# Half of the weight remainders of the two token mixers computed on POOL instead of VectorE

## The chip, the cores and the metric

The kernel runs on one core of one Trainium2 chip. The metric is device time in microseconds (us) of one execution, the median of several runs; less is better. The profile names the engines PE (matrix products), PEld (its weight loads), DVE (VectorE), ACT (ScalarE), POOL (GpSimd) and SP (the queue that issues the DMAs).

## The reference

A decoder trunk of two layers on 256 tokens of width 1024, all in fp32. Each layer is a half-step gated feed-forward (FFN), a token mixer, and a second FFN; before each of the three stands an RMS norm whose gain, shift and output gate come from a conditioning vector.

```python
c_act = jax.nn.silu(c)
for l in range(DEPTH):                                   # DEPTH = 2
    mod = (c_act @ w_ada[l] + b_ada[l])[:, None, :]
    sh0, sc0, g0, sh1, sc1, g1, sh2, sc2, g2 = jnp.split(mod, N_MOD, axis=-1)
    h = _rmsnorm(x, norm_g[l, 0]) * (1.0 + sc0) + sh0
    x = x + 0.5 * g0 * _swiglu(h, ffn_w_gate[l, 0], ffn_w_up[l, 0], ffn_w_down[l, 0])
    h = _rmsnorm(x, norm_g[l, 1]) * (1.0 + sc1) + sh1
    x = x + g1 * _token_mix(h, w_in[l], w_out[l], ...)
    h = _rmsnorm(x, norm_g[l, 2]) * (1.0 + sc2) + sh2
    x = x + 0.5 * g2 * _swiglu(h, ffn_w_gate[l, 1], ffn_w_up[l, 1], ffn_w_down[l, 1])
return _rmsnorm(x, final_g)
```

`_token_mix` projects h by w_in, runs three groups of heads beside each other (a spatial gating unit, a differential attention, and a sparse attention with a compressed and two windowed branches), joins their outputs and projects them by w_out.

## The kernel before

Tokens lie on the free axis (256 of them), the model axis on the 128 partitions in 8 chunks. PE gets fp32 accuracy out of three float32r products: each weight tile comes from memory as a raw fp32 tile `wst`, ACT copies it to a float32r tile `wh` (line 207), and DVE subtracts the two (line 211) so that `wl` holds what the copy rounded away. A product of 128 output rows is then, for each of 8 chunks, wh times the high part of h, wh times its low part, and wl times the high part: 24 products of 256 columns. A weight tile is 128x1024 (512 KB) in most places; the values of the sparse attention use tiles of 840 and 560 columns (`w_in_vs`).

`split` issues the load, the copy and the subtraction. The pools let it run ahead of PE: 5 raw tiles, 6 wh, 6 wl. SP issues the loads in a fixed order, each when its raw tile is free, so when the subtraction that last read it is done.

Each mixer (`mix`) takes 29 splits: 14 tiles of w_in with weights stationary (`ws_u`, `ws_in`), 4 + 3 tiles with tokens on the partitions (`xs_in`), and 8 tiles of w_out. The order of PE within a mixer is written out by hand (`MIX_ORDER`, one list of parts per layer); the orders of DVE, ACT, POOL and SP are set by a scheduler when the program is built, and each engine runs its own list strictly in order. On DVE the mixer also does the softmax maxima and reciprocals (533, 541), the rotary sums (512, 522), the scalings of the probabilities (692 to 698, 906 to 917), the norm (272, 276), and `acc` (192, 194): the products of w_ada with the conditioning vector, a chunk of 128x512 at a time, which fill free places of DVE ahead of the next FFN. POOL does nothing after four small memsets at the start.

In the trace the first mixer lies at about 222 to 376 us and the second at 757 to 900. Both have the same three parts: a head (projections of the compressed branch, norm, values; to 252 and 788), a middle (attention; to 340 and 860), and the output projection at the end (`ps_out`).

Of the kernel before, what the change touches and what calls it, by code (L numbers as in the profile page):

```python
# [10 lines left out]
F32 = mybir.dt.float32  # L11
# [7 lines left out]
T = 256  # L19
# [16 lines left out]

# [1 line left out]
def _cols(spec):  # L38
    off, m = 0, {}
    for name, n in spec:  # L40
        m[name] = slice(off, off + n)
        off += n
    return m, off


NW = 16         # products that warm the tensor engine while the first loads arrive
BUFS = dict(acc=2, ad=4, sm=4, t1k=9, u=27, wh=6, wl=6, wst=5)
LATE = 4        # tiles of the first FFN that run before it loads modulation weights
# order of the parts of the token mixer, layer by layer
MIX_ORDER = ["""  # L50
# [7 lines left out]
"""]  # L58
NE = 2          # gate/up tiles (and pairs of w_in tiles) that run before the norm is known
NS = 7          # gate/up tiles of the first FFN that are accumulated while w_ada arrives  # L60
UW = 2 * T + 2
# [50 lines left out]
def trunk_kernel(ctx: ExitStack, tc: tile.TileContext, A, depth=DEPTH, nf=NF, fsplit=FSPLIT):  # L112
    nc = tc.nc
# [7 lines left out]
    up = pool("u", BUFS["u"])  # L121
# [5 lines left out]

# [1 line left out]
    par = sing.tile([P, depth * NLC + 16], F32, name="par")  # L129
# [4 lines left out]
    h = sing.tile([P, KD, 2 * T], F32R, name="h")  # L134
# [21 lines left out]

# [1 line left out]
    def ada_cols(l, m, ks, ps):  # L158
        dst = mod[l][:, m, ks]
        nc.vector.tensor_add(dst, ps, lp(l, "bada")[:, m * 8 + ks.start:m * 8 + ks.stop])  # L160
        s, kind = divmod(m, 3)
        if kind == 1:
            nc.vector.scalar_tensor_tensor(out=gs[l][:, s, ks], in0=dst, scalar=1.0,
                                           in1=lp(l, "ng")[:, s * 8 + ks.start:s * 8 + ks.stop],
                                           op0=ALU.add, op1=ALU.mult)
        elif kind == 2:
            nc.vector.tensor_scalar_mul(hg[l][:, s, ks], dst, 1.0 if s == 1 else 0.5)
# [29 lines left out]

# [1 line left out]
    def load(src, cols, pool=wst, tag="wst"):  # L199
        st = pool.tile([P, cols], F32, name="wst", tag=tag)  # L200
        nc.sync.dma_start(st, src)
        return st

    def split(src, cols, mid=None):
        st = load(src, cols)
        wh = whp.tile([P, cols], F32R, name="wh", tag="wh")
        nc.scalar.activation(wh, st, AF.Copy)  # L207
        if mid:
            mid()
        wl = wlp.tile([P, cols], F32R, name="wl", tag="wl")  # L210
        nc.vector.tensor_sub(wl, st, wh.bitcast(F32))  # L211
        return wh, wl
# [7 lines left out]

# [1 line left out]
    sqs = [None]  # L222
# [12 lines left out]

    # brings the table of Sqrt in behind an instruction
    def sqrt_table(after):
        warm = sm.tile([P, 1], F32, name="warm", tag="ub")
        with tc.issue_after(after.ins):
            nc.scalar.activation(warm, ones, AF.Sqrt)  # L240

    # 1/rms of every token, broadcast over the partitions
    def rms_tokens():
# [34 lines left out]

    # x * gain before the norm is known: parts of a chunk, and the shift as two more columns
    def u_shift(l, s):  # L280
        sh = mod[l][:, 3 * s, :]
        nc.scalar.activation(ut[:, :, T], sh, AF.Copy)
        nc.vector.tensor_sub(ut[:, :, T + 1], sh, ut[:, :, T].bitcast(F32))
# [6 lines left out]

    # W^T (x * gain) and, per row, W^T shift
    def ws_u(src):
        wh, wl = split(src, KD * P)
        ps = psm.tile([P, T + 2], F32, name="ps_wu", tag="mm")
        for k in range(KD):
            s = slice(k * P, (k + 1) * P)
            mm(ps, wh[:, s], ut[:, k, :T + 2], start=(k == 0), stop=False)
            mm(ps[:, :T], wh[:, s], ut[:, k, T + 2:], start=False, stop=False)
            mm(ps, wl[:, s], ut[:, k, :T + 2], start=False, stop=(k == KD - 1))
        return ps  # L300
# [7 lines left out]

    # out[128 rows of W, T] of W^T h: weights stationary
    def ws_h(ps, wh, wl, ncol=P):  # L310
# [21 lines left out]

# [1 line left out]
    def swiglu_mul(pg, pu, gb=None, ub=None, pool=tp, tag="t1k"):  # L334
# [19 lines left out]

    # the first gate/up tiles, chunk by chunk of the model axis as its modulation arrives
    def startup(ns):
# [36 lines left out]
        with tc.manual_schedule(engines={mybir.EngineType.PE, mybir.EngineType.DVE, mybir.EngineType.Activation}):  # L393
            wt = up.tile([P, 2 * T], BF16, name="wt", tag="u")
            nc.vector.memset(wt, 0.0)
            wps = psw.tile([P, 2 * T], F32, name="ps_warm", tag="w")
            for _ in range(NW):
                mm(wps, wt[:, :P], wt, True, True)
# [51 lines left out]
    def ffn(l, w, ada_f, ada_d, nxt):  # L450
# [3 lines left out]
        if l == 0 and w == 0:  # L454
            raw += startup(min(NS, nf))
            act = [None] * len(raw)
        else:
            rb = rms_rows()
            for k in range(KD):
                h_chunk(l, s, k, rb)  # L460
            for f in range(min(NE, nf)):
                pg, gb = apply_r(ws_u(gate[f]), rb)
                pu, ub = apply_r(ws_u(upw[f]), rb)
                act.append(swiglu(pg, pu, gb, ub))
        f0 = len(act)
        late = LATE if raw else 0
        slots = spread(ada_f, nf - f0 - late)
# [39 lines left out]

# [1 line left out]
    def rope_sum(dst, z, cos, sin, n=T, b=None):  # L509
# [19 lines left out]

    # exp of score segments [128, n, keys] in PSUM, with the sums of their rows  # L530
    def softmax_seg(ps, n, name):
# [12 lines left out]
    def mix(l, ada, nxt):  # L544
        WI = A["w_in_ws"]
        pse = [ws_u(WI[l, 0])]
        r = rms_tokens()
        pse.append(ws_u(WI[l, 1]))
        rb = rms_bcast(r)
        early = [apply_r(p, rb) for p in pse]  # L550
        for k in range(KD):
            h_chunk(l, 1, k, rb)
        early += [apply_r(ws_u(WI[l, n]), rb) for n in (12, 13)]
        lam_init = 0.8 - 0.6 * math.exp(-0.3 * l)
        # lambda of the differential attention, on every partition
        lt = sm.tile([P, 64], F32, name="lt", tag="lt", bufs=1)
# [27 lines left out]

        # -- projections, tokens on partitions --
        def xs_in(src, width, kspl):
# [16 lines left out]
        def rope_q(dst, n, cos, sin, zb=None):  # L603
            z, b = zb if zb else (ws_in(WI[l, n]), None)
            rope_sum(dst, z, cs(cos), cs(sin), b=b)

        def rope_k(tiles, n, cos, sin, sel0):
            t = tp.tile([P, T], F32, name="ksum", tag="t1k")
            rope_sum(t, ws_in(WI[l, n]), cs(cos), cs(sin))
            for e, (ku, g) in enumerate(tiles):  # L610
# [5 lines left out]

        # -- gate of the spatial gating unit (before the norm is known) --
        uu = unit("ug")
# [6 lines left out]

        # -- blocks of the compressed branch: columns (group, block), position code, position code --
        a_t = []
# [13 lines left out]

        # -- values of the differential attention, v of the gating unit --
        pss = xs_in(A["w_in_gd"][l], 512, (2, 2, 2, 2))
# [3 lines left out]
        for i in range(NI):  # L647
            v = dvu[:, i * T:(i + 1) * T]
# [15 lines left out]

        # -- differential attention --
        osb, da_p = [], []
# [91 lines left out]

        # -- spatial gating unit --
        def gating():  # L760
# [33 lines left out]

        # -- compressed keys and values --
        hsb, hid = [], []
# [38 lines left out]

        # -- sparse attention --
        qu = [unit("qn") for _ in range(2)]
# [3 lines left out]
        gate = sm.tile([P, NI, 24], F32, name="gate", tag="gate", bufs=1)  # L841
# [120 lines left out]
        def w_out(m, c0, c1):  # L962
            if c0 == 0:
                wh, wl = split(A["w_out"][l, m], KD * P)
                ps = psw.tile([P, T], F32, name="ps_out", tag="w")
                wo[m] = wh, wl, ps
            wh, wl, ps = wo[m]
            for c in range(c0, c1):
                s = slice(c * P, (c + 1) * P)
                mm(ps, wh[:, s], yt[c][:, :T], c == 0, False)  # L970
                mm(ps, wh[:, s], yt[c][:, T:], False, False)
                mm(ps, wl[:, s], yt[c][:, :T], False, c == KD - 1)
            if c1 == KD:
                return add_out(l, 1, m, ps, nxt, 1)
# [31 lines left out]
        for m in range(2, KD):  # L1006
            if ada:
                ada_next()
            if m == KD - 2:
                ada_flush()  # L1010
                sqrt_table(after)
                u_shift(*nxt)
            after = w_out(m, 0, KD)

# [1 line left out]
    def halves(l, ms):  # L1016
# [28 lines left out]

# [1 line left out]
def _w_in_columns():  # L1047
# [33 lines left out]
def _layout(inp, depth, nf):  # L1081
    g = {k: np.asarray(v) for k, v in inp.items()}
    ns = min(NS, nf)
    o = {}
# [57 lines left out]
```

## Time and profile before

| | |
|---|---|
| median of 3 runs | 1096.6 us (1095.26 to 1096.73) |
| span of the profiled execution, first to last instruction | 1093.7 us |
| median less span (the profiled execution's own time is not listed; this is taken as what lies around its span) | 2.9 us |
| first mixer, 222 to 376 | 154 us: DVE busy 130.8, ACT 106.2, PE 140.3 |
| second mixer, 757 to 900 | 143 us: DVE busy 118.7, ACT 101.4, PE 136.3 |
| subtraction of line 211 | 332 times, 391.0 us in all, 58 of them in the two mixers |

An engine's busy time is that in which at least one of its instructions ran. The times of PE overlap and their ends are modelled, so a high busy share of PE does not say that it had no room. Where the text speaks of the chain, it means the profile's chain of waits: followed back from the last instruction, at each step to what released it.

### The profile page before, as it was taken

To read this page: it belongs to the slowest core of one execution; us is meant where nothing else is said; L and a number is where in the kernel's file an instruction comes from. 1 tells how busy PE (TensorE), PEld (TensorE's weight loads), DVE (VectorE), ACT (ScalarE), POOL (GpSimd) and SP (SyncE) were. 2 spreads that over 40 slices of the span, in tenths; PEclk is the share of its full clock that TensorE was granted. 3 is DMA by queue.
4 is the path that set the end of the run, shared out by engine and by line. 5 is a ranking of instruction groups with operands and counts; after the bars stand their busy time and mean duration, and the time that the engine had idled before them with its cause. 6 is when DMAs were issued, how large, how long until landed. Compare 5 with 4: busy or idle time off the path is not lost.

```text
span 1093.7 us, 20684 instructions
## 1 busy us (share of the span) xinstructions
PE 1060.2 (97%) x7928; PEld 970.2 (89%) x7928; DVE 850.8 (78%) x1573; ACT 624.7 (57%) x1320; POOL 0.2 (0%) x4
## 2 busy tenths in 40 slices
PE   8999999998988999999999999999999999999997
PEld 5899998887775999999899999988787699999986
DVE  3479999767997999887879878786799878555563
ACT  4365545666675865554556555455867766454441
POOL 0000000000000000000000000000000000000000
PEclk8999999999998999999999999999999999999999
DMA  8868988944835679997866888785555145555551
GB/s 330 295 238 339 355 326 310 324 160 132 320 130 181 221 243 343 341 312 252 280 230 231 318 277 297 263 312 197 180 184 184 58 154 174 188 180 187 174 159 39
DMA packets 73827, 257.55 MB, mean 235 GB/s; under 512 B 8320, under 2 KB 9728, under 8 KB 73728
## 3 DMA queue, kind: packets, MB, share of 16 engines
q1 hardware_dynamic: 73728, 256.23, 67.3%
q8 instruction: 62, 1.02, 0.4%
q14 instruction: 37, 0.30, 0.1%
HBM read 255.14 MB, written 1.05 MB: 234 GB/s over the span
## 4 chain that ended last, share of the span: by engine, by line
PE 83%; DVE 10%; ACT 5%; issue 1%; DMA 1%; SPq 0%; DVEq 0%; ACTq 0%
PE ps_ws L219 41%; PE ps_dn L219 23%; PE ps_wu L219 5%; PE ps_fst L219 4%; PE ps_out L219 4%; DVE wl L211 2%; DVE rt L512 2%; PE ps_y L219 1%; DVE mx L533 1%; ACT cmpa L637 1%; PE ps_ada L176 1%; PE ps_row L219 1%; DVE acc L194 1%; ACT pn L538 1%; DMA ast<-in_w_ada_dram 1%
## 5 line engine op out<-in xcount | busy, mean ns | idle before, releaser
L207 ACT ACTIVATE wh<-wst 128x1024 fp32r<-128x1024 f32 (+2 forms) x332 | 340.3, 1030 | 289.0 <-PE ps_ws L219 101.9
L219 PE MATMUL ps_ws<-h,wh 128*128 128x256 f32 x2720 | 488.9, 283 | 6.9 <-DVE dv L650 6.1
L211 DVE TENSOR_TENSOR wl<-wst,wh 128x1024 fp32r<-128x1024 f32 (+2 forms) x332 | 391.0, 1183 | 118.2 <-ACT wh L207 116.9
L219 PEld LDWEIGHTS ps_ws<-h,wh 128*128 128x128 f32 x2720 | 419.6, 190 | 9.2 <-DVE dv L650 7.0
L219 PE MATMUL ps_ws<-h,wl 128*128 128x256 f32 x1360 | 383.2, 282 | 0.3 <-DVE wl L211 0.3
L219 PEld LDWEIGHTS ps_ws<-h,wl 128*128 128x128 f32 x1360 | 258.0, 190 | 0.5 <-DVE wl L211 0.5
L219 PE MATMUL ps_dn<-act,wh 128*128 128x512 f32 (+1 forms) x726 | 249.1, 391 | 0.0
L219 PE MATMUL ps_dn<-act,wl 128*128 128x256 f32 x704 | 197.7, 281 | 0.0
L194 DVE SCALAR_TENSOR_TENSOR acc<-ast,cact,acc 128x512 f32<-128x512 f32 x224 | 167.3, 747 | 2.5
L219 PEld LDWEIGHTS ps_dn<-act,wh 128*128 128x128 f32 x726 | 134.9, 188 | 30.3
L219 PEld LDWEIGHTS ps_dn<-act,wl 128*128 128x128 f32 x704 | 133.2, 189 | 0.0
L219 PE MATMUL ps_wu<-ut,wh 128*128 128x258 f32 (+1 forms) x320 | 60.1, 286 | 0.9 <-DVE ut L288 0.9
L219 PEld LDWEIGHTS ps_wu<-ut,wh 128*128 128x128 f32 x320 | 49.7, 189 | 1.4 <-DVE ut L288 1.3
L342 DVE TENSOR_TENSOR a<-ps_ws,sg 128x256 f32<-128x256 f32 x75 | 31.6, 421 | 21.8 <-PE ps_ws L219 21.5
L219 PE MATMUL ps_out<-y,wh 128*128 128x256 f32 x256 | 47.4, 286 | 0.2 <-DVE xT L325 0.2
L215 ACT ACTIVATE act<-a 128x256 fp32r<-128x256 f32 x88 | 35.2, 408 | 21.1 <-DVE a L342 19.1
L219 PE MATMUL ps_fst<-h,wh 128*128 128x256 f32 x224 | 43.4, 297 | 1.8 <-ACT h L275 1.8
L219 PE MATMUL ps_wu<-ut,wl 128*128 128x258 f32 x160 | 45.0, 282 | 0.0
L219 PEld LDWEIGHTS ps_fst<-h,wh 128*128 128x128 f32 x224 | 35.5, 198 | 6.9 <-issue 4.5
L219 PEld LDWEIGHTS ps_out<-y,wh 128*128 128x128 f32 x256 | 39.8, 191 | 1.6 <-issue 1.0
L325 DVE SCALAR_TENSOR_TENSOR xT<-ps_dn,hg,xT 128x256 f32<-128x256 f32 x63 | 30.2, 480 | 12.0 <-PE ps_dn L219 11.3
L226 ACT ACTIVATE sq<-xT 128x256 f32<-128x256 f32 x48 | 19.9, 414 | 33.7 <-DVE xT L325 33.2
(203 smaller groups left out, 1115.1 us busy)
## 6 DMA issues: line engine op xcount, KB each, us to landing
ast<-in_w_ada_dram SPq DMA_DIRECT2D x144, 512.0 KB, 5.3
wst<-in_w_gate_dram SPq DMA_DIRECT2D x81, 512.0 KB, 4.5
wst<-in_w_up_dram SPq DMA_DIRECT2D x81, 512.0 KB, 4.3
wst<-in_w_down_dram SPq DMA_DIRECT2D x64, 512.0 KB, 4.5
wst<-in_w_in_ws_dram SPq DMA_DIRECT2D x28, 512.0 KB, 3.8
wst<-in_w_down_dram SPq DMA_DIRECT2D x32, 384.0 KB, 4.0
wst<-in_cmp_w_dram SPq DMA_DIRECT2D x16, 512.0 KB, 5.8
wst<-in_w_out_dram SPq DMA_DIRECT2D x16, 512.0 KB, 4.8
```

The source lines that it names most:

```text
L176: nc.tensor.transpose(ps[:, c * P:(c + 1) * P], acc[:, c * P:(c + 1) * P], ident)
L194: nc.vector.scalar_tensor_tensor(out=acc, in0=st[:, k2, :], scalar=col, in1=acc, op0=ALU.mult, op1=ALU.add)
L207: nc.scalar.activation(wh, st, AF.Copy)
L211: nc.vector.tensor_sub(wl, st, wh.bitcast(F32))
L215: nc.scalar.activation(dst[:, :T], src, AF.Copy)
L219: nc.tensor.matmul(out, lhsT, rhs, start=start, stop=stop, skip_group_check=True)
L226: square = nc.scalar.activation(sq, xT[:, k, :], AF.Square)
L325: nc.vector.scalar_tensor_tensor(out=xT[:, m, :], in0=ps[:, half * T:(half + 1) * T], scalar=hg[l][:, s, m:m + 1], in1=xT[:, m, :], op0=AL ...
L342: nc.vector.tensor_mul(a, pu, sg)
L512: nc.vector.tensor_mul(out, z, t)
L533: nc.vector.tensor_reduce(mx[:, :n], ps, axis=AX.X, op=ALU.max, negate=True)
L538: nc.scalar.activation(pt[:, g * w:(g + 1) * w], ps[:, g, :], AF.Exp, bias=mx[:, g:g + 1], accum_out=su[:, g:g + 1])
```

## The change

From the first line of a mixer to its last, `split` hands every second subtraction to POOL (`nc.gpsimd`) instead of DVE. The counter runs through the whole program, FFN splits included, so the first mixer starts with POOL and gives it 15 of its 29, the second starts with DVE and gives POOL 14. The copies on ACT, the loads and the arithmetic are the same. Outside the mixers nothing goes to POOL. The other lines of the file differ in comments only, which shifts line numbers by up to 7 (211 becomes 216).

```diff
+    shared = [False, 0]
...
     def split(src, cols, mid=None):
         st = load(src, cols)
         wh = whp.tile([P, cols], F32R, name="wh", tag="wh")
         nc.scalar.activation(wh, st, AF.Copy)
         if mid:
             mid()
         wl = wlp.tile([P, cols], F32R, name="wl", tag="wl")
-        nc.vector.tensor_sub(wl, st, wh.bitcast(F32))
+        shared[1] += 1
+        low = nc.gpsimd if shared[0] and shared[1] % 2 else nc.vector
+        low.tensor_sub(wl, st, wh.bitcast(F32))
         return wh, wl
...
     def mix(l, ada, nxt):
         WI = A["w_in_ws"]
+        shared[0] = True
         pse = [ws_u(WI[l, 0])]
...
             after = w_out(m, 0, KD)
+        shared[0] = False
```

On POOL, which had nothing there, the program of the change has these rows, in the order of the two mixers (`wl` is the remainder, `wst` the raw tile, `wh` its copy; the ISA row stands ahead of the first of them and waits for nothing):

```order
L216 ISA
L216 TENSOR_TENSOR wl<-wst,wh 128x1024 x7
L216 TENSOR_TENSOR wl<-wst,wh 128x840
L216 TENSOR_TENSOR wl<-wst,wh 128x560
L216 TENSOR_TENSOR wl<-wst,wh 128x1024 x13
L216 TENSOR_TENSOR wl<-wst,wh 128x840
L216 TENSOR_TENSOR wl<-wst,wh 128x1024 x6
```

They are 29 subtractions, 15 of the first mixer and 14 of the second.

On DVE, in the middle of the first mixer (about 313.8 us in the trace of before), at the softmax of one head pair of the sparse attention (`pn`, `mx`, `rc`, `cf`) beside that of the compressed branch (`ce`, `cmx`), the program before has:

```order
L194 SCALAR_TENSOR_TENSOR acc<-ast,cact,acc 128x512
L211 TENSOR_TENSOR wl<-wst,wh 128x1024
L194 SCALAR_TENSOR_TENSOR acc<-ast,cact,acc 128x512
L541 RECIPROCAL rc<-su 128x4
L862 TENSOR_TENSOR ce<-ps_cs,cst 128x60
L904 TENSOR_TENSOR cf_3877<-rc,gate 128x4
L533 TENSOR_REDUCE mx<-ps_s_3835 128x2
L906 TENSOR_TENSOR pn_3869<-pn_3869,cf_3877 128x512
L865 TENSOR_REDUCE cmx<-ce 128x4
L211 TENSOR_TENSOR wl<-wst,wh 128x1024
L541 RECIPROCAL rc<-su 128x2
L866 TENSOR_TENSOR ce<-ce,cmx 128x60
```

The changed program has at the same place:

```order
L194 SCALAR_TENSOR_TENSOR acc<-ast,cact,acc 128x512
L216 TENSOR_TENSOR wl<-wst,wh 128x1024
L868 TENSOR_TENSOR ce<-ps_cs,cst 128x60
L871 TENSOR_REDUCE cmx<-ce 128x4
L546 RECIPROCAL rc<-su 128x4
L872 TENSOR_TENSOR ce<-ce,cmx 128x60
L910 TENSOR_TENSOR cf_3877<-rc,gate 128x4
L538 TENSOR_REDUCE mx<-ps_s_3835 128x2
L912 TENSOR_TENSOR pn_3869<-pn_3869,cf_3877 128x512
L876 TENSOR_REDUCE csu<-ce 128x4
L878 RECIPROCAL crc<-csu 128x4
L192 TENSOR_SCALAR acc<-ast,cact 128x512
```

One of the two subtractions and one `acc` are gone from in front of the softmax instructions, and the compressed branch's (`ce`) come earlier. Between the first `dv` copy and the last `y` of a mixer, DVE has 16 subtractions before and 8 after, in either layer, and 32 and 16 `acc` instructions both before and after.

On DVE, in the output projection of the first mixer (from about 359 us), one row a tile for `xT` (the residual), `sqa` (its squares) and `ut` (the next FFN's input), the program before has:

```order
L194 SCALAR_TENSOR_TENSOR acc<-ast,cact,acc 128x512
L211 TENSOR_TENSOR wl<-wst,wh 128x1024
L233 TENSOR_TENSOR sqa<-sqa,sq 128x256
L288 SCALAR_TENSOR_TENSOR ut<-xT,gs_105,ut 128x256
L325 SCALAR_TENSOR_TENSOR xT<-ps_out,hg_107,xT 128x256
L211 TENSOR_TENSOR wl<-wst,wh 128x1024
L233 TENSOR_TENSOR sqa<-sqa,sq 128x256
L288 SCALAR_TENSOR_TENSOR ut<-xT,gs_105,ut 128x256
L211 TENSOR_TENSOR wl<-wst,wh 128x1024
L325 SCALAR_TENSOR_TENSOR xT<-ps_out,hg_107,xT 128x256
```

The changed program has there:

```order
L194 SCALAR_TENSOR_TENSOR acc<-ast,cact,acc 128x512 x2
L238 TENSOR_TENSOR sqa<-sqa,sq 128x256
L293 SCALAR_TENSOR_TENSOR ut<-xT,gs_105,ut 128x256
L216 TENSOR_TENSOR wl<-wst,wh 128x1024
L330 SCALAR_TENSOR_TENSOR xT<-ps_out,hg_107,xT 128x256
L216 TENSOR_TENSOR wl<-wst,wh 128x1024
L238 TENSOR_TENSOR sqa<-sqa,sq 128x256
L293 SCALAR_TENSOR_TENSOR ut<-xT,gs_105,ut 128x256
L330 SCALAR_TENSOR_TENSOR xT<-ps_out,hg_107,xT 128x256
L194 SCALAR_TENSOR_TENSOR acc<-ast,cact,acc 128x512
```

One subtraction of the three has left this piece. The order of PE differs in one place only, where the head's first products and the statistics of the norm stand a few rows apart from where they stood.

## Rows read from the trace of the kernel before

**Rows 1.** The page, part 1: busy us and share of the span.

```profile
PE 1060.2 (97%) x7928; PEld 970.2 (89%) x7928; DVE 850.8 (78%) x1573; ACT 624.7 (57%) x1320; POOL 0.2 (0%) x4
```

**Rows 2.** The chain of waits by line, 252 to 340, then 788 to 860.

```profile
by line: DVE rt L512 12.5%; DVE wl L211 9.9%; DVE mx L533 9.0%; DVE acc L194 7.8%; issue 6.4%; PE ps_ws L219 6.3%; ACT pd L538 5.1%; PE ps_s L219 4.7%; PE ps_y L219 2.5%; DVE rc L541 2.2%; DVE pn L906 2.0%; ACT pn L538 2.0%; ACT kd L612 1.9
...
by line: PE ps_ws L219 22.5%; DVE wl L211 13.9%; DVE mx L533 8.5%; DVE rt L512 8.4%; DMA wst<-in_w_out_dram 4.8%; PE ps_d L219 4.2%; issue 3.6%; ACT pn L538 2.7%; DVE pd L693 2.1%; DVE y L216 2.0%; ACT pd L538 1.9%; DVE rc L541 1.8%; DVE ac
```

**Rows 3.** Windows: us, busy us by engine, granted clock, DMA share, GB/s.

```profile
222.00:252.00 30.00, 25.60 (x159) 22.86 (x159) 18.97 (x41) 23.66 (x41) 0.00 (x0) 0.96 0.35 119
252.00:340.00 88.00, 78.75 (x591) 62.96 (x590) 83.35 (x222) 58.06 (x175) 0.00 (x0) 0.98 0.61 211
356.00:376.00 20.00, 20.00 (x169) 19.98 (x167) 19.90 (x39) 16.92 (x43) 0.00 (x0) 1.00 0.68 222
788.00:860.00 72.00, 68.65 (x492) 57.25 (x491) 67.83 (x183) 49.68 (x140) 0.00 (x0) 0.97 0.49 170
878.00:900.00 22.00, 21.64 (x178) 21.14 (x177) 19.02 (x33) 15.52 (x26) 0.00 (x0) 1.00 0.49 168
```

**Rows 4.** Groups of DVE, 252 to 340, then one of 788 to 860.

```profile
L194 DVE SCALAR_TENSOR_TENSOR acc<-ast,cact,acc 128x512 f32<-128x512 f32 x21 | 15.6, 741 | 0.0
L211 DVE TENSOR_TENSOR wl<-wst,wh 128x1024 fp32r<-128x1024 f32 x12 | 14.5, 1215 | 0.1
...
L211 DVE TENSOR_TENSOR wl<-wst,wh 128x840 fp32r<-128x840 f32 x2 | 2.1, 1034 | 0.1
L693 DVE SCALAR_TENSOR_TENSOR pd<-pd,rc 128x256 f32<-128x256 f32 x4 | 1.9, 477 | 0.0
...
L192 DVE TENSOR_SCALAR acc<-ast,cact 128x512 f32<-128x512 f32 x3 | 1.4, 480 | 0.0
L692 DVE TENSOR_SCALAR pd<-pd,rc 128x256 f32<-128x256 f32 x4 | 1.4, 345 | 0.0
...
L211 DVE TENSOR_TENSOR wl<-wst,wh 128x560 fp32r<-128x560 f32 x1 | 0.7, 734 | 0.0
...
L211 DVE TENSOR_TENSOR wl<-wst,wh 128x1024 fp32r<-128x1024 f32 x12 | 14.6, 1217 | 0.1
```

**Rows 5.** Groups of ACT, 252 to 340: copying a raw tile.

```profile
L207 ACT ACTIVATE wh<-wst 128x1024 fp32r<-128x1024 f32 x12 | 12.6, 1056 | 3.7 <-PE ps_ws L219 3.4
```

**Rows 6.** DVE in order of time, from 316.7: start us, us, instruction.

```profile
316.71 0.16 DVE L904 TENSOR_TENSOR cf<-rc,gate 128x4 f32<-128x4 f32 x1
316.79 0.68 DVE L533 TENSOR_REDUCE mx<-ps_s 128x2 f32<-128x512 f32 x1
317.39 0.68 DVE L906 TENSOR_TENSOR pn<-pn,cf 128x512 f32<-128x512 f32 x1
317.99 0.21 DVE L865 TENSOR_REDUCE cmx<-ce 128x4 f32<-128x60 f32 x1
318.12 1.22 DVE L211 TENSOR_TENSOR wl<-wst,wh 128x1024 fp32r<-128x1024 f32 x1
```

**Rows 7.** POOL's only instructions in the whole run, grouped by shape.

```profile
L1132 POOL MEMSET const-float32-0.0<- 128x1 f32 x1 | 0.1, 98 | 0.2 <-issue 0.2
```

**Rows 8.** DVE, then ACT, in time order: head of the first mixer.

```profile
231.75 2.06 DVE L272 SCALAR_TENSOR_TENSOR tn<-xT,gs,rb 128x256 f32<-128x256 f32 x5
...
236.90 1.27 DVE L276 SCALAR_TENSOR_TENSOR h<-tn,mod,h 128x256 fp32r<-128x256 f32 x3
...
238.56 0.41 DVE L306 TENSOR_TENSOR zu<-ps_wu,rb 128x256 f32<-128x256 f32 x1
...
238.83 1.28 ACT L623 ACT_TABLE_LOAD   x1
240.12 0.91 ACT L623 ACTIVATE ug<-zu,ub 128x256 f32<-128x256 f32 x2
```

**Rows 9.** Waits of the DMA queue, 222 to 376: us in total, times, longest.

```profile
SPq L201 <- DVE wl L211: 57.7, 20, 9.5
```

**Rows 10.** Chain of waits in order of time, 860 to 900: the output projection.

```profile
879.56 17.52 PE ps_out L219 x144
```

## The prediction

> **What bounds the kernel now.** The page's busy times come first: PE is busy 97% of the span, DVE 78%, ACT 57%, POOL not at all [rows 1]. That is an average over FFNs, where PE is full, and mixers, where it isn't, and only the mixers are changed. So the windows come next. In the middle of the first mixer, 252 to 340, DVE is busy 83.35 of 88 us (95%) and in that of the second, 788 to 860, 67.83 of 72 (94%); PE leaves 9.3 and 3.4 us, ACT 30 and 22 [rows 3]. DVE is the fullest engine there by the first of them and nearly level with PE by the second. The chain of waits of the same two stretches then says what a microsecond of DVE is worth: the subtractions `wl` of line 211 stand on it with 9.9% of 88 us, 8.7 us, and with 13.9% of 72, 10.0 us [rows 2]. Their busy time there is 14.5 + 2.1 + 0.7 = 17.3 us for 15 of them, and 17.4 in the second mixer, where the full tiles take 14.6 us and the three smaller ones what they take in the first [rows 4]. So 0.50 and 0.57 of what DVE spends on them ends up in the time; the rest lies beside chains that go through ACT and PE. The head of a mixer is not DVE's (18.97 of 30 us in the first), and in the output projection PE is full: 20.00 of 20 us, with DVE at 19.90 in the first mixer and 19.02 of 22 in the second [rows 3].
>
> **What leaves DVE.** Of the 29 subtractions that move, 16 are in the two middles (8 of 16 in either by the order of DVE). At 17.3 / 15 = 1.155 us each that is 9.24 us of DVE per mixer [rows 4]. In the time, by the shares above: 9.24 x 0.50 + 9.24 x 0.57 = 4.6 + 5.3 = **9.9 us off**, if nothing else changes. The `acc` instructions, 0.74 us each [rows 4], are as many in the middles as before, so the freed places are not filled with others' work.
>
> **What one costs on POOL.** The trace has no subtraction on POOL, only memsets of one element, 0.1 us [rows 7]. It can't be bounded by these. Below stands DVE's own 1.22 us, with both operands read at once [rows 4]. Above, an engine that takes two reads and a write one after the other, each at the pace of ACT's copy of the same tile, 1.056 us, would need 3.2 [rows 5]. I take 2 x 1.056 = **2.1 us**: two operands, one after the other; POOL has nothing in this kernel that suggests it is as wide as DVE. Its own time is hidden where PE takes the tiles more slowly than POOL makes them. In the output projection 144 products take 17.52 us, so a tile of 24 takes 2.92 [rows 10], and POOL has every second one: 5.84 us for 2.1. In the middles tiles are taken more slowly still. The remainder of a tile on POOL comes 0.9 us later, and its raw tile is free 0.9 us later for the next load. SP waits for these 57.7 us in 20 waits in the first mixer [rows 9]; that is a queue that runs ahead, with five raw tiles, and DMA moves data 0.61 of the middle and 0.68 of the projection [rows 3], so I count nothing. Were that cover gone, it would be 29 x 0.9 = 26 us.
>
> **What POOL does to DVE.** This decides the sign. Look at DVE's own rows: with one tensor operand, 256 more columns cost 480 - 345 = 135 ns, 0.53 ns a column; with two, 741 - 477 = 264 ns, 1.03 [rows 4]. With one operand DVE gets through twice as fast, so it seems to have two ways into the memory, and an instruction with two operands, or a fast one with one, uses both. Nothing in the trace shows POOL beside it. The cost lies between none (POOL has a way of its own) and POOL's whole time (they share one, and DVE waits at its first instruction that needs both until POOL is done). I take the second as the likelier, less what DVE can still do: instructions with an operand in PSUM, or reductions. In the rows from 316.7 such an instruction (`mx`, 0.68; `cmx`, 0.21) stands between any two that need both (`cf`, `pn`, `wl`) [rows 6], and counting the moments inside the others, after which the next gap follows, DVE has about 0.4 us of free work when POOL starts; this is an estimate. So DVE stands for 2.1 - 0.4 = 1.7 us per POOL instruction. Behind it in its queue then wait `mx` and `rc`, for which ACT's exponentials wait, and after those PE's transposes. Per mixer's middle 8 x 1.7 = 13.6 us of DVE, in the time 13.6 x 0.50 + 13.6 x 0.57 = 6.8 + 7.8 = **14.6 us on**.
>
> The page "SBUF — State Buffer" of the Trainium skill, section "Who interferes with whom", states just this: DVE and GpSimd share a port pair as an exclusive lock, and a DVE instruction with two SBUF inputs contends with a GpSimd one that reads SBUF; the second to issue blocks until the first ends. No run here shows it yet. By this rule the change costs, and without it it gains 9.9 us; the rule speaks against the change. The page "GPSIMD Engine Reference", section "Elementwise — side-by-side cycle accounting", gives 4497 ns for a two-input add of 2048 columns; an estimate from it for 1024 is 2.25 us, and the sum below would come to 1106.6 by it.
>
> **Head and tail.** In the first output projection DVE has no room (19.90 of 20), and POOL has three tiles whose time lies there: 3 x (1.7 - 1.22) = 1.4 us on. In the second the 3 us of room take it [rows 3]. In the heads DVE makes the norm in one run of two-operand instructions, from 231.75 to 238.2, and `zu` behind it ends at 238.97; ACT needs that for `ug` at 240.12, after a table load, so 1.15 us are spare [rows 8]. One POOL subtraction falls into that run per mixer and holds it up by 2.1 us: 2.1 - 1.15 = 0.95, twice 1.9 us.
>
> **Sum.** -9.9 + 14.6 + 1.4 + 1.9 = +8.0 us. The profiled span of 1093.7 becomes 1101.7, and with the 2.9 us between span and median **1104.6 us**, against 1096.6 (+0.7%). With POOL at 3.2 us a block is 2.8: 8 x 2.8 x 1.07 = 24.0, the tail 4.7, the heads 4.1, in all +22.9, 1119.5. With 1.22 it is 0.82: 7.0, no tail (DVE would stand 0.82 and save 1.22), heads 0.1, in all -2.8, 1093.8.
>
> **Rivals.**
> - POOL has its own way, or shares it so finely that DVE hardly notices: DVE is just relieved, -9.9, **1086.7 us**. For it speaks that the moved work is on the chain and that POOL is idle; against it DVE's two rates. It decides if blocks fall below 9.9 / (16 x 0.535) = 1.16 us per POOL instruction in the middles. That point is 0.54 us under my 1.7, so it is near. Chance 0.32.
> - The two cancel: POOL's price lies low (about 1.6 us, so a block of 1.2), or DVE is slowed by half and not held: within 2.2 us of **1096.6**. Chance 0.17.
> - DVE goes first, POOL waits: then DVE keeps its gain, but POOL's remainders come late, and PE waits for them in the projection, where tiles follow each other most closely. Eight tiles late by one tile's time of 2.92 us [rows 10] are 23.4 us: -9.9 + 23.4 = +13.5, **1110.1**. Against it speaks the run-ahead of six wl tiles. Chance 0.07.
> - That the change does nothing is excluded: POOL has the 29 rows in its order.
>
> **How the numbers follow.** My forecast, DVE held by POOL, has 0.44; its own range is 1099 to 1114. Within 0.2% (2.2 us, about what a measurement of this kernel can tell from no change) lies the third case. Faster 0.32, same 0.17, slower 0.44 + 0.07 = 0.51. The range for 8 in 10 must take in the relieved case and the dearer POOL: **1087 to 1117**, which leaves out what is beyond the full gain below, and a POOL price near 3.2 us above, about 0.1 each.
>
> **What the new profile would show.** If I am right: POOL rows of 2 us and more in the middles; beside them DVE's two-operand rows longer than before (or idle gaps before them), `acc` above 0.74 and remaining `wl` above 1.22, while `mx`, with its operand in PSUM, keeps 0.68; DVE busy in the middles not lower although 8 subtractions left; both mixers longer, 154 and 143 us before. The first rival would show DVE's rows unchanged, DVE busy down by 9 us per middle, and the mixers shorter by about 5 each. The last would show POOL rows far longer than 2.1 and PE waiting for `wl` by POOL in `ps_out`. Wrong I would be above all by the length of one POOL subtraction and by whether DVE stands beside it.

## The result, and the profile of the changed kernel

| | before | changed |
|---|---|---|
| median, us | 1096.62 (4 runs) | 1131.26 (1130.83 to 1132.11, 4 runs) |
| ratio, with its 95% interval | | 1.0321 (1.0306 to 1.0336) |
| profiled execution: span, us | 1093.7 | 1129.6 |
| mean granted clock | 0.984 | 0.973 |

The change costs 34.6 us. The prediction had the sign, with 8.0 us, and its range ended at 1117. Below, times against the kernel before are its median of the same series of runs, 1097.1 to 1097.8 us. In every execution whose span is listed the time is 1.7 to 1.9 us above the span, not 2.9. So the profiled execution of the kernel before, whose own time is not listed, will have lain about 1.1 us under its median, which is why the spans differ by 35.9 us and the medians by 34.6.

Part 1 of the page answers to [rows 1]: PE is busy for 13.1 us longer with the same 7928 products, and for 22.8 us more of the span it does nothing (56.3 for 33.5).

```profile
PE 1073.3 (95%) x7928; PEld 978.0 (87%) x7928; DVE 857.8 (76%) x1544; ACT 624.1 (55%) x1320; POOL 71.7 (6%) x33
```

The windows of the same parts of the program answer to [rows 3] (us, then busy us of PE, PEld, DVE, ACT and POOL, granted clock, DMA share, GB/s):

```profile
222.00:254.00 32.00, 25.92 (x159) 22.84 (x158) 19.86 (x38) 23.65 (x43) 8.22 (x4) 0.97 0.36 119
254.00:355.00 101.00, 85.80 (x589) 66.50 (x588) 86.85 (x219) 57.98 (x175) 19.40 (x8) 0.91 0.55 187
370.00:390.00 20.00, 19.29 (x162) 19.07 (x161) 19.76 (x36) 15.16 (x40) 2.84 (x1) 1.00 0.62 197
...
809.00:895.00 86.00, 74.46 (x494) 60.88 (x495) 74.54 (x179) 48.83 (x139) 17.56 (x7) 0.91 0.46 165
912.00:932.00 20.00, 19.78 (x162) 19.45 (x163) 17.53 (x29) 14.78 (x25) 2.41 (x1) 1.00 0.49 159
```

The middles are 101 and 86 us long instead of 88 and 72. Between the same products of PE in both traces they lose 12.9 and 14.0 us, the two heads 1.7 and 3.8, the first output projection 2.7 and the second nothing. DVE is no longer full in them: it idles 14.2 and 11.5 us where it idled 4.7 and 4.2. PE's granted clock is 0.91 in both, where it was 0.98 and 0.97.

POOL in the changed kernel, grouped by shape over the whole run; a subtraction of 1024 columns takes 2.4 us where nothing else holds it (median 2397 ns):

```profile
L216 POOL TENSOR_TENSOR wl<-wst,wh 128x1024 fp32r<-128x1024 f32 x26 | 65.0, 2501 | 838.6 <-ACT wh L210 827.0 <-PE ps_d L224 9.6 <-DVE xT L330 2.0
L216 POOL TENSOR_TENSOR wl<-wst,wh 128x840 fp32r<-128x840 f32 x2 | 4.5, 2241 | 2.8 <-ACT wh L210 2.8
L216 POOL TENSOR_TENSOR wl<-wst,wh 128x560 fp32r<-128x560 f32 x1 | 2.0, 2013 | 3.6 <-ACT wh L210 3.6
```

What a POOL instruction does to DVE is seen by laying both in order of time, POOL first, then DVE, in the first middle:

```profile
288.16 2.56 POOL L216 TENSOR_TENSOR wl<-wst,wh 128x1024 fp32r<-128x1024 f32 x1 [14.69 <-ACT wh L210]
291.83 2.79 POOL L216 TENSOR_TENSOR wl<-wst,wh 128x1024 fp32r<-128x1024 f32 x1 [1.12 <-ACT wh L210]
```

```profile
288.39 2.87 DVE L194 SCALAR_TENSOR_TENSOR acc<-ast,cact,acc 128x512 f32<-128x512 f32 x1
291.18 0.47 DVE L699 SCALAR_TENSOR_TENSOR pd<-pd,rc 128x256 f32<-128x256 f32 x1
...
292.31 0.20 DVE L697 TENSOR_SCALAR rc<-rc,nlam 128x1 f32<-128x1 f32 x1
292.43 2.34 DVE L698 TENSOR_SCALAR pd<-pd,rc 128x256 f32<-128x256 f32 x1
```

`acc`, 0.74 us in [rows 4], stands 2.87 us and ends 0.54 us after POOL; `pd` of line 698 (692 before), 0.35 us in [rows 4], stands 2.34 and ends 0.15 us after POOL. `rc`, 128x1, passes. How such a hold reaches PE is seen at 316.7 (POOL, DVE, ACT, PE; the bracket is the idle time ahead and what ended it):

```profile
316.66 2.49 POOL L216 TENSOR_TENSOR wl<-wst,wh 128x1024 fp32r<-128x1024 f32 x1 [22.04 <-ACT wh L210]
...
316.85 2.32 DVE L917 TENSOR_TENSOR cf<-rc,gate 128x2 f32<-128x2 f32 x1
319.09 0.68 DVE L538 TENSOR_REDUCE mx<-ps_s 128x2 f32<-128x512 f32 x1
...
320.21 0.41 DVE L752 COPY drb<-dr 128x512 f32<-128x512 f32 x1
...
319.86 0.47 ACT L543 ACTIVATE pn<-ps_s,mx 128x256 f32<-128x256 f32 x1 [2.03 <-DVE mx L538]
...
320.77 1.08 PE L760 MATMUL ps_rb<-cst,drb 128*128 128x128 f32 x4 [2.90 <-DVE drb L752]
```

In the kernel before the same rows stand at 305.8 (those of [rows 6] at 316.71 are of a later step); DVE, then PE:

```profile
305.84 0.15 DVE L911 TENSOR_TENSOR cf<-rc,gate 128x2 f32<-128x2 f32 x1
```

```profile
307.60 0.63 PE L754 MATMUL ps_rb<-cst,drb 128*128 128x128 f32 x4 [0.77 <-DVE drb L746]
```

`cf` has two columns, takes 0.15 us before and stands 2.32 us. Behind it in DVE's queue are `mx`, for which ACT's exponential waits 2.03 us, and `drb`, for which PE waits 2.90 instead of 0.77. Summed over both mixers, every DVE row beside a POOL row less the median of the same row before, DVE is held for 36.1 us by 29 POOL instructions, 21.1 of them by the 16 in the middles.

The section "Who interferes with whom" of the page "SBUF — State Buffer" in the Trainium skill says that both engines share a port pair, which whoever comes first keeps for its whole instruction. The rows agree: the held row does its work once POOL's has ended, whether it has two columns or 512.

### The profile page after: what moved, and what is told of

Its sections match the earlier page's. It is cut to its first block, busy times and chain, and to the rows that moved or that the text cites. A ratio compares the mean times of both kernels' runs of the same rounds, so it can differ in the third digit from the quotient of the medians.

```text
span 1129.6 us, 20713 instructions
## 1 busy us (share of the span) xinstructions
PE 1073.3 (95%) x7928; PEld 978.0 (87%) x7928; DVE 857.8 (76%) x1544; ACT 624.1 (55%) x1320; POOL 71.7 (6%) x33
## 5 line engine op out<-in xcount | busy, mean ns | idle before, releaser
L216 DVE TENSOR_TENSOR wl<-wst,wh 128x1024 fp32r<-128x1024 f32 (+1 forms) x303 | 358.2, 1187 | 123.7 <-ACT wh L210 122.6
L224 PEld LDWEIGHTS ps_ws<-h,wh 128*128 128x128 f32 x2720 | 421.0, 190 | 15.7 <-DVE dv L656 10.0
L194 DVE SCALAR_TENSOR_TENSOR acc<-ast,cact,acc 128x512 f32<-128x512 f32 x224 | 173.4, 775 | 3.9 <-DMA ast<-in_w_ada_dram 1.4
L216 POOL TENSOR_TENSOR wl<-wst,wh 128x1024 fp32r<-128x1024 f32 (+2 forms) x29 | 71.4, 2466 | 844.9 <-ACT wh L210 833.3
L231 ACT ACTIVATE sq<-xT 128x256 f32<-128x256 f32 x48 | 19.9, 415 | 38.7 <-DVE xT L330 38.3
```

Of the source, the lines that this page charges most:

```text
L194: nc.vector.scalar_tensor_tensor(out=acc, in0=st[:, k2, :], scalar=col, in1=acc, op0=ALU.mult, op1=ALU.add)
L216: low.tensor_sub(wl, st, wh.bitcast(F32))
L224: nc.tensor.matmul(out, lhsT, rhs, start=start, stop=stop, skip_group_check=True)
L231: square = nc.scalar.activation(sq, xT[:, k, :], AF.Square)
```

## The experiments

Unless said otherwise, the edits are made in the changed kernel, in the branch of `split` that hands a subtraction to POOL. "Not busy" is the span less PE's busy time. "1.2 GHz" is how long the records of the granted clock show the lower level between the start of the first mixer and the end of the second. "Held" is the sum just described; two rows that stand at once can be counted once or twice, which moves the small sums by up to 1.4 us. All columns but the ratio are of the one profiled execution, which for twice on DVE and for the middles lay 3.8 and 4.6 us under the median of its kernel.

| kernel | ratio to before (95%) | span | PE busy | not busy | 1.2 GHz | held |
|---|---|---|---|---|---|---|
| before | 1 | 1093.7 | 1060.2 | 33.5 | 20.5 | 0 |
| left out | 1.0000 (0.9984 to 1.0016) | 1092.6 | 1054.5 | 38.1 | 10.2 | 0 |
| write only | 0.9988 (0.9978 to 0.9998) | 1094.7 | 1055.7 | 39.0 | 13.7 | 1.4 |
| late without reads | 1.0038 (1.0024 to 1.0051) | 1100.5 | 1062.0 | 38.5 | 27.3 | 8.4 |
| one read | 1.0106 (1.0089 to 1.0123) | 1108.4 | 1068.3 | 40.1 | 37.5 | 10.1 |
| half the columns | 1.0084 (1.0069 to 1.0099) | 1105.5 | 1061.4 | 44.1 | 20.5 | 14.6 |
| quarters | 1.0174 (1.0159 to 1.0189) | 1115.9 | 1064.5 | 51.4 | 27.3 | 27.0 |
| changed | 1.0321 (1.0306 to 1.0336) | 1129.6 | 1073.3 | 56.3 | 47.8 | 36.1 |
| heads and tails | 1.0088 (1.0067 to 1.0109) | 1103.9 | 1061.5 | 42.4 | 23.9 | 15.0 |
| middles | 1.0253 (1.0232 to 1.0273) | 1117.8 | 1067.2 | 50.6 | 34.1 | 21.5 |
| twice on DVE | 1.0056 (1.0035 to 1.0077) | 1097.1 | 1058.4 | 38.7 | 20.5 | 0 |

### Left out: what is the relief worth?

```diff
+        if shared[0] and shared[1] % 2:
+            return wh, wh
         wl = wlp.tile([P, cols], F32R, name="wl", tag="wl")
```

> The 29 subtractions that the change moves to POOL are left out on every engine; the product that reads such a remainder reads the high part in its place, so this part of the computation is missing and PE's work is unchanged. It shows what relief of VectorE alone is worth, with no POOL work at all. Theory (the prediction's first term): the relief is about 9.9 us in the two middles and some 2 to 4 us in heads and tails, so about 1083 to 1088 us; the 35 us between the kernel before and the changed one are then more than 40 us of harm by POOL. Rival (relief is worth nothing, since VectorE is waited for at a few places that do not move): 1094 to 1098 us. Second rival (the harm is the new order of the instructions on VectorE and not POOL): 1110 us or more.

1096.32 us, ratio 1.0000. DVE does 28 us less in all. Between the same products of PE, the middles of [rows 3] have it at 77.23 of 87.3 us (before 83.35 of 88) and 65.33 of 75.9 (67.83 of 72). The windows, and the chain of waits in them, for [rows 2]:

```profile
250.30:337.60 87.30, 78.90 (x592) 63.33 (x590) 77.23 (x216) 58.29 (x173) 0.00 (x0) 0.98 0.63 217
781.80:857.70 75.90, 70.03 (x494) 58.60 (x492) 65.33 (x181) 49.98 (x140) 0.00 (x0) 0.96 0.54 193
```

```profile
by line: PE ps_ws L225 18.0%; DVE acc L194 11.0%; DVE mx L539 9.2%; DVE rt L518 7.4%; ACT pn L544 4.9%; ACT pd L544 4.2%; issue 4.1%; ACT kd L619 2.9%; DVE wl L217 2.7%; PE ps_y L225 2.4%; DVE rc L547 2.0%; PE ps_out L225 1.6%; DVE acc L192
```

```profile
by line: PE ps_ws L225 24.0%; PE ps_s L225 11.9%; DMA ast<-in_w_ada_dram 10.1%; DVE rt L518 7.0%; DVE mx L539 6.5%; DVE wl L217 4.5%; PE ps_d L225 4.0%; ACT pd L544 3.7%; DVE acc L194 2.7%; issue 2.7%; PE ps_da L225 1.4%; PE ps_rb L761 1.4%
```

The rival holds: the relief is worth nothing that can be measured (at most 1.8 us). The middles, from which 4.6 and 5.3 us were to go, are 0.7 us shorter and 3.9 us longer. `wl` has mostly left the chain, 2.4 and 3.4 us of it for 8.7 and 10.0 before; other rows have come in its place. In the first middle these are PE's products `ps_ws` (15.7 us for 5.5) and `acc` (9.6 for 6.9), in the second the products `ps_s` (9.0 us) and a load of w_ada (7.7 us).

### Twice on DVE: what does more DVE time cost?

```diff
+        for _ in range(2 if shared[0] and shared[1] % 2 else 1):
+            nc.vector.tensor_sub(wl, st, wh.bitcast(F32))
```

> No POOL work: each of the 29 subtractions that the change moves is made on VectorE, twice in a row. That adds 29 x 1.22 = 35.4 us to VectorE, as much as the 36 us or so by which its rows stand longer beside POOL in the changed kernel, but as one piece at the subtraction's own place. Theory A (time taken from VectorE in a mixer costs its full length, wherever it falls): 1126 to 1133 us. Theory B (it costs about half, as the prediction's shares of the chain had it, and the rest of the loss comes from where POOL's holds strike, ahead of softmax and rotary rows): 1107 to 1116 us.

1102.69 us, +0.56% or 6 us, below both theories: 34.5 us more of subtractions, at the places that the program's own order gives them, cost a sixth of their length. DVE's fullness, from which the prediction began, doesn't set the time. So the 36.1 us for which POOL holds DVE cost what they do by where they strike, not as so many microseconds of DVE.

### Write only, and late without reads: the order, the lateness, or the reading?

The first kernel writes a memset of zero over the low tile; the second has this branch:

```diff
+            nc.gpsimd.tensor_sub(wl[:, :1], st[:, :1], wh[:, :1].bitcast(F32))
+            nc.gpsimd.memset(wl.bitcast(F32), 0.0)
+            nc.gpsimd.memset(wl.bitcast(F32), 0.0)
+            nc.gpsimd.tensor_sub(wl[:, :1], st[:, :1], wh[:, :1].bitcast(F32))
```

> POOL writes zeros into the 29 low tiles in place of subtracting (the remainders are left out; PE's products with them are still made). POOL reads nothing and only writes 128x1024. Theory (VectorE is held by a POOL instruction that reads two operands, as the rows of the changed kernel show it for the whole length of each subtraction): a POOL write alone holds VectorE little or not at all, so 1083 to 1097 us. Rival (any POOL instruction on SBUF holds VectorE for its length): by the memset's rate in the profile of before the holds are some 0.4 to 0.6 of those of the subtraction, so 1105 to 1118 us.

> POOL makes the 29 low tiles as late as the subtraction would, and holds the raw tile as long, but reads only one column: a subtraction of 128x1, two memsets of zero over the tile (about 0.96 us each by the run that only writes) and the subtraction of 128x1 again; so the remainders are left out but for a column. Theory (the loss is VectorE held by POOL's reading): 1094 to 1100 us. Rival (the loss is the lateness of wl and of the raw tile, which the prediction counted at nothing and put at 26 us at most): 1115 to 1130 us.

The first kernel's writes wait for no load and no copy, so its tiles come early; the second has them as late as the change. Both keep the changed kernel's order on ACT and PE, and on DVE but for an `acc` at one or two places. They take 1095.68 us, as the theory had it, and 1101.35, 1.4 us over its range and far below the rival's. This excludes the new order as the cause, and leaves for lateness 4 us over the kernel before, 5.7 over the write-only one (in part the second kernel's own holds, 8.4 us). That the tiles hold zeros is not what makes these two fast: without the subtractions PE multiplies by the high part instead, and the time is the same. The rows of 316.7, in the write-only kernel, DVE, then PE:

```profile
307.78 0.15 DVE L919 TENSOR_TENSOR cf<-rc,gate 128x2 f32<-128x2 f32 x1
...
308.97 0.42 DVE L754 COPY drb<-dr 128x512 f32<-128x512 f32 x1
...
309.54 0.63 PE L762 MATMUL ps_rb<-cst,drb 128*128 128x128 f32 x4 [0.76 <-DVE drb L754]
```

`cf` has its 0.15 us again, and PE waits 0.76 us for `drb` instead of 2.90.

### One read, half the columns, quarters: how long must a hold be?

POOL copies `wh` (one operand), subtracts half of the columns, or subtracts in four pieces; the last:

```diff
+            q = cols // 4
+            for i in range(0, cols, q):
+                nc.gpsimd.tensor_sub(wl[:, i:i + q], st[:, i:i + q], wh[:, i:i + q].bitcast(F32))
```

> POOL copies the high part into the low tile in place of subtracting: one operand read and one tile written, 29 times (the remainders are left out, the products with these tiles are still made). The order of all engines is that of the changed kernel but for a few grouped rows. Theory (any POOL instruction that reads this memory holds VectorE's fast and two-operand rows until it ends): POOL's rows last 1 to 2 us and the loss is in proportion to them, 1108 to 1125 us, with VectorE rows that end together with POOL's. Rival (only two operands read at once hold VectorE; a copy is like the memset): 1094 to 1100 us.

> POOL subtracts only the first half of the columns of its 29 tiles and writes zeros into the other half (so half of these remainders are left out). Same order on VectorE, ACT and PE. POOL's reading is halved, about 1.2 us an instruction. Theory of proportion (a microsecond of hold costs about a microsecond): half of the 34 us, 1111 to 1117 us. Rival (short holds are taken up by the slack that the runs without reading showed, and long ones cost more than their length through PE's clock): below 1108 us.

> The changed kernel, with each of POOL's 29 subtractions cut into four of a quarter of the columns. Same order on VectorE, ACT and PE, same results; POOL's total time a little longer. Theory (the hold lasts until the one POOL instruction ends, then VectorE gets its turn): a held row stands 0.6 to 0.8 us and not 2.4, fewer of the holds strike a row that PE waits for, and a good part of the 34 us goes: 1103 to 1118 us. Rival (VectorE is held again at once by the next piece, so that POOL's total time is what counts): 1128 to 1140 us.

1110.10, 1107.87 and 1117.96 us, with the order of the changed kernel (the copy with the few `acc` rows of the write-only one). One operand read is enough to hold DVE: the theory of any reading, in its range. Half the columns cost 9 us, which is the rival's range, not the proportion's: the holds are 0.40 of the changed kernel's, the loss 0.26, and the time at 1.2 GHz is that of before. The quarters lie at the upper end of their theory. POOL's groups of the copy, the halves and the quarters:

```profile
L216 POOL CAST wl<-wh 128x1024 fp32r<-128x1024 f32 x26 | 29.6, 1137 | 851.4 <-ACT wh L210 834.5 <-PE ps_d L226 13.5 <-DVE xT L332 3.4
```

```profile
L218 POOL TENSOR_TENSOR wl<-wst,wh 128x512 fp32r<-128x512 f32 x26 | 35.5, 1366 | 43.9 <-ACT wh L210 43.4 <-DVE xT L334 0.5
```

```profile
L218 POOL TENSOR_TENSOR wl<-wst,wh 128x256 fp32r<-128x256 f32 x104 | 86.9, 866 | 806.7 <-ACT wh L210 778.8 <-DMA ast<-in_w_ada_dram 13.8 <-PE ps_h L228 8.5
```

The row `cf` of the same place is 0.99 us beside the copy (its instruction there takes 1.20), 1.23 beside the half, 0.69 beside a quarter, 2.32 beside the whole: it stands for the rest of one POOL instruction. Between two quarters DVE gets its turn, so a single hold is short, but there are more of them, 27.0 us in all for 36.1.

### Middles, heads and tails: where?

The 16 subtractions of the middles go to POOL in one kernel (the seventh to fourteenth that `split` hands over in the first mixer, the sixth to thirteenth in the second), the other 13 in the other.

> Only the 16 subtractions of the two middles go to POOL (8 in each mixer), the other 13 stay on VectorE. Theory (VectorE is full in the middles, holds cost most there): 22 to 29 of the 34 us stay, 1118 to 1126 us. Rival (every POOL subtraction costs the same 1.2 us): 16 of 29, 1114 to 1117 us. Second rival (the heads, where the norm's rows are held, weigh most): below 1110 us.

> The complement: only the 13 subtractions of heads and output projections go to POOL. Theory: 1101 to 1108 us. Rival (same cost everywhere): 13 of 29, 1112 to 1115 us. The prediction had 3.3 us less the relief there, about 1098 to 1100 us. If the losses of this kernel and of the one for the middles add up to much less than 34 us, what is missing comes from both together.

1124.18 and 1106.61 us: 27 and 9.5 us, both in the theory's range. They add up to 36.5, near the 34.6 of both together. A POOL subtraction costs 1.7 us in a middle and 0.7 elsewhere.

### Fillers: what part is PE's clock?

In all eleven kernels of the table PE's busy time less half of the time at 1.2 GHz is 1048 to 1051 us. So what PE is busier by is its lower clock, to within 3 us: from the write-only kernel to the changed one, which share their order, 17.6 us of PE's busy time and 17.3 in which it isn't busy. To see what the first half is worth, products whose results are overwritten were put ahead of waits in the changed kernel and in the kernel before.

```diff
+    def fill(ps, n):
+        for _ in range(n):
+            mm(ps, identb, negb[:, None, :].to_broadcast([P, 4, P]), True, False)
...
+            fill(ops_, 20 if l == 1 and a == 1 else 0)
```

> The changed kernel, with 60 filler products of 128x512 (results overwritten) put on PE ahead of five of its long waits: 14 and 20 ahead of the waits for dv at 251.5 and for at at 857.2, 10 ahead of drb at 320.8, 16 in each layer after the exponentials of lambda. POOL's and VectorE's work is unchanged. Theory (about 27 us more of the mixers run at a granted clock near 0.5 than before, because PE now waits longer; part of the loss is the clock): the half-speed stretches behind these waits go away and the time falls by 8 to 14 us, to 1117 to 1123 us. Rival (the loss is the blocked VectorE alone, and the clock falls in time that PE would have waited anyway): no change, 1129 to 1133 us, or a few us more by the fillers themselves.

> The kernel before with the same 60 filler products at the same places. Its half-speed stretches in the mixers are 20.5 us in all. Theory of the clock: up to 10 us of work is given back at most, less the fillers that do not fit into a wait: 1088 to 1095 us. Rival (its waits are too short for the clock to cost anything, and the fillers only stand in the way): 1097 to 1103 us.

1135.47 us (ratio 1.0345, 1.0325 to 1.0365) and 1110.20 (1.0125, 1.0107 to 1.0142). The theory's gain is in neither, and the kernel before is slower than even the rival had it. But the totals don't decide: the fillers (76, since the group of 16 stands in both layers) add 12.9 us of PE's busy time to the kernel before, which the expectation had not counted, and DVE's order differs from the changed kernel's in places. In the changed kernel the time at 1.2 GHz fell from 47.8 to 30.7 us. Two stretches with the same products in both tell more. The first is behind the wait for `qn`, in the changed kernel and with fillers:

```profile
300.48 3.78 PE L224 MATMUL ps_s<-kn,qn 128*128 128x256 f32 x6 [3.84 <-DVE qn L527]
...
307.55 0.65 PE L224 MATMUL ps_o<-at,dv 128*64 128x256 f32 x4 [0.34 <-DVE rt L517]
```

```profile
304.31 1.99 PE L224 MATMUL ps_s<-kn,qn 128*128 128x256 f32 x6 [0.81 <-DVE qn L527]
...
310.46 0.76 PE L224 MATMUL ps_o<-at,dv 128*64 128x256 f32 x6 [2.37 <-DVE rt L517]
```

At 2.4 GHz the six products take 1.99 us instead of 3.78, but PE then waits 2.37 us for `rt` instead of 0.34: of the faster clock 0.9 us is left (6.15 for 7.07 from row to row). The second is at the end of the first middle, where PE, once it has started, waits for nobody:

```profile
356.93 1.28 PE L224 MATMUL ps_y<-pt,vsw 128*64 128x128 f32 x12 [1.11 <-ACT pt L944]
...
365.69 0.38 PE L886 MATMUL ps_ct<-cst,ce 128*30 128x128 f32 x2
```

```profile
361.55 1.09 PE L224 MATMUL ps_y<-pt,vsw 128*64 128x128 f32 x12 [1.11 <-ACT pt L952]
...
367.14 0.38 PE L893 MATMUL ps_ct<-cst,ce 128*30 128x128 f32 x2
```

The same products take 8.76 us there and 5.59 with fillers, where the clock stays at 2.4 GHz: 3.2 us, all of it kept. So the clock costs its full price where PE runs through and little where the next wait is for DVE. How much of the 17.6 us a full clock would give back in all stays open. That it counts fits two kernels of nearly one order: the copy holds DVE less than the half columns (10.1 us for 14.6), but has 17 us more at 1.2 GHz and a span that is 2.9 us longer; the mean granted clock is 0.974 to 0.977 in all runs of the copy and 0.980 to 0.983 in all of the half columns. An estimate comes from the 45 runs of the kernel before in these series, with clocks of 0.980 to 0.989: their time falls by 0.56 us for each 0.001 of clock, which is 2.2 us less at 1.2 GHz and 1.1 us less of PE's busy time. So about half of the clock's price was in the time, which would be some 9 of the 17.6 us; no edit set these runs apart, so they show no cause.

## Why the prediction missed

**What bounds the kernel, and the relief of 9.9 us: the step that failed first.** That DVE is busy 95% of the middles and that `wl` stands on the chain with half its time [rows 2, 3] was read rightly; that taking away a microsecond of it gives half a microsecond back doesn't follow. Leaving the 29 subtractions out gave 0 (at most 1.8 us), POOL writing in their place gave 1.3, and doubling them cost 6 for 34.5. The chain without them shows why: PE's products and a load move into the place of `wl`, and the middles do not get shorter. This step alone would have made the forecast 1114.5 us, still inside its range; what took the time out of it is the clock, below.

**POOL's price, 2.1 us: nearly right.** 2.4 us alone, 2.47 in the mean of 29, between the bounds of 1.22 and 3.2. The estimate from the Trainium skill's page "GPSIMD Engine Reference", section "Elementwise — side-by-side cycle accounting", 2.25 us, was nearer.

**DVE held, 1.7 us each: the mechanism right, the size too high.** `acc` and the remaining `wl` are longer (2.87 and up to 2.04 us), `mx` keeps 0.68, DVE's busy time in the middles is not lower (86.85 and 74.54): all as the last part of the prediction had it. But a hold in the middles is 21.1 / 16 = 1.32 us for a POOL row of 2.47 there: for 1.1 us of it DVE did other work or had none, not 0.4. The point that the first rival named, 1.16, was near, and decided nothing, since the gain that it was weighed against wasn't there. The terms for holds, 14.6 + 1.4 + 1.9 = 17.9 us, are close to the 17.3 us by which PE is less busy than in the write-only kernel; in the kernel with POOL in the middles alone that is 11.6, with heads and tails alone 3.4, for 14.6 and 3.3 predicted. In heads and tails this agreement is luck: DVE was held there for 15.0 us, at other places than the prediction's.

**PE's clock: the term that was missing, and the second step that failed.** Nothing in the sum said that PE, when it waits longer, runs at 1.2 GHz afterwards. [Rows 3] had the granted clock of 0.98 and 0.97 in the middles. PE's busy time grew by 13.1 us over the kernel before and by 17.6 over the write-only one. The sum with the measured terms: 1.0 (span of the write-only kernel over before) + 17.3 + 17.6 = 35.9 us, the whole difference of the spans. This is a count of PE's time by what it did, not by cause; a part of the 17.6 would be waiting for DVE at a faster clock.

**Head and tail, 3.3 us:** 9.5 measured. In the trace of the kernel with POOL there alone, between the same products as before, the first head loses 2.1 us, the first output projection 2.0, the second head 6.3 and the second projection nothing. The run of `tn` of [rows 8] was held as described, and `ug`'s table load came at 240.32 for 238.83, 1.5 us for the 0.95 taken. The delay came through ACT, whose rows `h` wait for `tn`, and not through `zu`, from which the 1.15 us of spare time was read. In the second head PE waits for `dv` 5.7 us, for 2.2 before. In the first output projection of the changed kernel POOL has one subtraction, at 374.61, and not three; it holds an `acc` for 2.0 us.

**Lateness at nothing: held,** within the 4 to 5.7 us above. PE waits for no remainder of POOL's anywhere in the trace, so the rival in which DVE goes first falls, and SP's waits for both engines' `wl` in the first mixer come to 63.7 us in 20, for 57.7 in 20 [rows 9] (222 to 390):

```profile
SPq L201 <- POOL wl L216: 39.9, 11, 7.0
...
SPq L201 <- DVE wl L216: 23.8, 9, 6.1
```

**The rivals.** POOL with its own way is what the write-only kernel made real, and it takes 1095.68 us, not the 1086.7 that this rival was priced at: even without any hold there was nothing to gain. So the chance of 0.32 for faster stood on the relief alone. That the two cancel failed with it.

## What to carry to other kernels

An engine's busy share and its share of the chain don't say what relieving it is worth: a run that simply leaves the work out does, before anything is moved. POOL work that reads SBUF is not free beside DVE: it holds a DVE row of the kinds named below, two columns as much as 512, for the rest of POOL's instruction, and what counts is who waits behind that row. If it must be, short pieces are better (about half of the loss here). Where PE waits longer, look at its granted clock behind the wait and count that time too.

## What the runs showed of the hardware

- Held beside a POOL instruction that reads: DVE rows with two operands in SBUF (`acc`, `cf`, `sqa`, `ce`, `tn`) and copies and one-operand scalings from SBUF to SBUF (`pd` 0.35 to 2.34 us, `cmpa` 0.17 to 2.13). Not held, at the same moments: reductions, reciprocals, rows with an operand in PSUM (`rt`, `zu`), and scalings of a single column (`rc`), all within 0.02 us of their length before.
- A POOL write alone holds fewer. Two-operand rows pass a memset unchanged (`acc`, `cf`, `sqa`, `qn`, `vg`), but one-operand scalings stand until it ends, as two rows of `pn`, 0.60 us without it, in the kernel that is late without reads:

```profile
308.24 0.95 POOL L217 MEMSET wl<- 128x1024 f32 x1
309.25 0.98 POOL L218 MEMSET wl<- 128x1024 f32 x1
...
308.72 1.65 DVE L926 TENSOR_SCALAR pn<-pn,cf 128x256 f32<-128x256 f32 x2
```

- POOL for 1024 columns: memset 0.96 us, copy 1.04 where nothing holds it (1.14 in the mean), subtraction 2.4; a quarter of the subtraction takes 0.77 us when four follow each other (3.06 in all at 314.3), not 0.6.
